# A decoder layer on one Trainium2 core: gate and up by Strassen's seven products

## The chip, the cores and the metric

The kernel runs on one core of one Trainium2 chip. The core has five engines that each run their own list of instructions in order and wait for each other by semaphores: TensorE (PE, matrix products), VectorE (DVE), ScalarE (ACT), GpSimd (POOL) and SyncE (SP), which here only issues transfers. The metric is the device time of one execution in microseconds (us), the median of three runs.

## The reference

One decoder layer on 1024 tokens of width 1024, all in float32: a sub-layer of three token mixers, then a SwiGLU sub-layer. Only SwiGLU is touched:

```
def swiglu(u, w1, w2):
    gate, up = jnp.split(u @ w1, 2, axis=-1)      # w1: 1024 x 5632
    return (jax.nn.silu(gate) * up) @ w2          # w2: 2816 x 1024
...
        u = x * (1.0 + sc2) + sh2
        h = swiglu(u, ffn_w1[l], ffn_w2[l])
        x = layer_norm(DEEPNORM_ALPHA * x + (1.0 + g2) * h, ln2_g[l], ln2_b[l])
```

## The kernel before

Every large product is made from float32 operands split in two parts, high and low: `split` (L106) lets ACT copy the operand to the product's number format (the high part, L107) and lets DVE subtract that from the operand (the low part, L108). A product of two such operands is three matmuls: high by high, high by low, low by high. One matmul is 128x128 weights against 512 columns.

The input of SwiGLU, `u2h` and `u2l`, stands transposed in SBUF: 8 tiles of 128 channels (k), each in two halves of 512 tokens. Gate and up are made in 22 row blocks of 128 hidden channels. For a block, `wblock` loads 1024x128 weights of gate and splits them, and the same for up; `dense` runs, for each k, 3 matmuls on each half of the tokens into a PSUM tile `pgu` of 128x1024. So a block has 2 x 8 x 3 x 2 = 96 matmuls, written from the helper's line L143. Then ACT makes silu of gate (L1073), DVE multiplies with up (L1075), and the block goes to DRAM as part of `s_h` (L1076). Three PSUM tiles named `o0` to `o2` take turns. Block 0 runs its two halves one after the other, since the second half of `u2h` comes last out of the layer norm ahead of it.

Then comes the second product (`accf`, L1114): two groups of 512 tokens, in each 22 steps of k, a step being 24 matmuls on one loaded and split row block of w2 (`w2raw`, L1099) and one of `s_h` (`hraw`, L1104). Its pool `f2a` is opened ahead of the loop over gate and up, with four buffers for the split parts. At its start five rows are spread over all partitions (`g2row`, `l2g`, `l2b`, `l1g`, `l1b`, 512 KB each, on ACT's queue), DVE scales two of them (L1085, L1086), four tiles `x1r` are loaded on SP's queue (L1120), and POOL multiplies and adds on them (L1121, L1122).

The order of the instructions on each engine is set when the program is built: by the order of the code, priorities and a scheduler. `tc.issue_after(last[-1])` ties each group of matmuls behind the one before it. The waits between engines come from which tiles an instruction reads and writes.

Of the kernel before, what the change touches and what calls it, by code (L numbers as in the profile page):

```python
# [17 lines left out]
P = 128  # L18
D = 1024
# [24 lines left out]
def trunk(ctx: ExitStack, tc: tile.TileContext, a: dict, out: bass.AP, scratch: dict):  # L44
# [125 lines left out]
    def half(h):  # L170
        return slice(h * HF, (h + 1) * HF)
# [906 lines left out]
    uctx.close()  # L1078
    with tc.tile_pool(name="f2", bufs=2, reuse_waits="tile") as f2, \
            tc.tile_pool(name="f2l", bufs=4, reuse_waits="tile") as f2l:  # L1080
# [6 lines left out]
        for grp in range(2):  # L1087
            hs = half(grp)
            acc = []
            for t in range(4):  # L1090
                if t < 3:
                    both = pso.tile([P, T], F32, name="accf", tag=f"o{(t + 1) % 3}")
                    acc.append([both[:, half(h)] for h in range(2)])
                else:
                    acc.append([pso.tile([P, HF], F32, name="accf", tag="t", bufs=2) for _ in range(2)])

# [80 lines left out]
```

## Time and profile before

| what | us |
|---|---|
| median of 3 runs | 2154.46 (2154.38 to 2156.28) |
| the profiled execution's own time | 2151.05 |
| its span, first to last instruction | 2149.2 |
| gate and up (`pgu`), first to last matmul's start | 1406.3 to 1885.9 |
| second product (`accf`), first to last matmul's start | 1886.1 to 2136.7 |

The profile is that of one execution. A timeline gives for each instruction when it began and how long it took; a matmul's duration overlaps the next one's, so that the pace of matmuls is read from their starts. In brackets stands how long the engine had stood idle before it, and which instruction released it.

### The profile page before, as it was taken

The numbers are of one execution on the slowest core, as the hardware profiler recorded it, in microseconds if no ns is written. First come the engines' busy times: TensorE is split into PE (matmuls) and PEld (weight loads), VectorE is DVE, ScalarE is ACT, GpSimd is POOL, SyncE is SP. The second block draws the span as 40 slices with busy tenths as digits, with TensorE's granted clock in tenths as the row PEclk, the third lists the DMA queues.
The fourth block names the chain that finished last, engine by engine and source line by source line (L and its number), as shares of the span: only waits on it lengthen the run. The fifth ranks groups of instructions, "written<-read, shape, count | busy, mean of one in ns | idle before, by whom it ended". The sixth has DMA issues, their size and how long they took to land.

```text
span 2149.2 us, 26441 instructions
## 1 busy us (share of the span) xinstructions
PE 2078.0 (97%) x10482; PEld 1637.5 (76%) x10482; DVE 1068.8 (50%) x1986; ACT 688.8 (32%) x1078; POOL 212.6 (10%) x251
## 2 busy tenths in 40 slices
PE   6999999999999999999999999999999999999897
PEld 4777777776777677777767887888888888888786
DVE  6584565645734766445674567532111111154755
ACT  3524323234124342534444324541111111124242
POOL 1101102001010000011121000000000000040803
PEclk9999989989989999999999999999999999999999
DMA  9111111211113454211112755243222222156361
GB/s 285 50 60 37 43 59 35 65 40 35 64 47 94 135 150 118 69 35 38 28 38 88 253 156 172 89 133 93 79 79 69 79 69 79 50 177 194 128 200 65
DMA packets 186923, 202.68 MB, mean 94 GB/s; under 512 B 9500, under 2 KB 144816, under 8 KB 186800
## 3 DMA queue, kind: packets, MB, share of 16 engines
q1 hardware_dynamic: 159216, 133.22, 21.0%
q10 hardware_dynamic: 26752, 66.69, 9.0%
q8 instruction: 82, 1.34, 0.3%
q0 software_dynamic: 832, 1.09, 0.2%
q14 instruction: 41, 0.34, 0.0%
HBM read 162.16 MB, written 38.81 MB: 94 GB/s over the span
## 4 chain that ended last, share of the span: by engine, by line
PE 78%; DVE 10%; issue 4%; ACT 4%; DMA 3%; POOL 1%; SPq 1%; ACTq 0%; DVEq 0%; POOLq 0%
PE pgu L143 22%; PE psd L143 21%; PE accf L1114 9%; PE pj L143 6%; PE woa L1024 3%; PE po L865 2%; PE pt L851 2%; DVE tw L473 1%; DVE TI L475 1%; PE pm L458 1%; PE pss L835 1%; PE pw L525 1%; PE pst L537 1%; PE pss L836 1%; DVE VS L705 1%
## 5 line engine op out<-in xcount | busy, mean ns | idle before, releaser
L143 PE MATMUL psd<-ul,wh 128*128 128x512 f32 x992 | 338.5, 412 | 2.0 <-DVE ul L274 2.0
L107 ACT ACTIVATE wh<-wraw 128x1024 fp32r<-128x1024 f32 (+1 forms) x127 | 124.2, 978 | 663.3 <-PE pgu L143 344.6
L143 PE MATMUL psd<-uh,wh 128*128 128x512 f32 x992 | 334.6, 409 | 0.7 <-ACT uh L272 0.5
L143 PE MATMUL psd<-uh,wl 128*128 128x512 f32 x992 | 332.9, 409 | 1.1 <-DVE wl L120 1.1
L108 DVE TENSOR_TENSOR wl<-wraw,wh 128x1024 fp32r<-128x1024 f32 (+1 forms) x127 | 142.1, 1119 | 214.5 <-ACT wh L107 212.2
L143 PEld LDWEIGHTS psd<-ul,wh 128*128 128x128 f32 x992 | 184.5, 192 | 45.1 <-issue 9.7
L143 PEld LDWEIGHTS psd<-uh,wh 128*128 128x128 f32 x992 | 185.8, 192 | 41.4 <-issue 6.8
L143 PEld LDWEIGHTS psd<-uh,wl 128*128 128x128 f32 x992 | 185.4, 192 | 40.2 <-issue 6.3
L143 PE MATMUL pgu<-oh,wl 128*128 128x512 f32 x352 | 137.2, 390 | 0.0
L143 PE MATMUL pgu<-ul,wh 128*128 128x512 f32 x352 | 137.2, 390 | 0.0
L143 PE MATMUL pgu<-uh,wl 128*128 128x512 f32 x352 | 137.2, 390 | 0.0
L143 PE MATMUL pgu<-uh,wh 128*128 128x512 f32 x352 | 137.2, 390 | 0.0
L143 PE MATMUL pgu<-oh,wh 128*128 128x512 f32 x352 | 137.1, 389 | 0.0
L143 PE MATMUL pgu<-ol,wh 128*128 128x512 f32 x352 | 137.1, 389 | 0.0
L1075 DVE TENSOR_TENSOR ht<-sg,pgu 128x1024 f32<-128x1024 f32 x22 | 26.9, 1221 | 198.8 <-PE pgu L143 179.4
L1114 PE MATMUL accf<-w2h,hh 128*128 128x512 f32 x352 | 116.4, 393 | 6.1 <-DVE t1f L1139 4.5
L1114 PE MATMUL accf<-w2l,hh 128*128 128x512 f32 x352 | 116.7, 395 | 1.2 <-DVE w2l L108 1.2
L1114 PE MATMUL accf<-w2h,hl 128*128 128x512 f32 x352 | 115.9, 392 | 0.0
L1121 POOL TENSOR_TENSOR x1r<-x1r,l1g 128x1024 f32<-128x1024 f32 x8 | 22.1, 2777 | 816.2 <-DVE l1g L1085 742.4
L108 DVE TENSOR_TENSOR w2l<-w2raw,w2h 128x1024 fp32r<-128x1024 f32 x44 | 65.2, 1484 | 37.6 <-ACT w2h L107 37.5
L1114 PEld LDWEIGHTS accf<-w2h,hh 128*128 128x128 f32 x352 | 66.6, 189 | 20.7 <-DVE t1f L1139 4.9
L1114 PEld LDWEIGHTS accf<-w2l,hh 128*128 128x128 f32 x352 | 66.9, 191 | 15.9 <-DVE w2l L108 2.1
(350 smaller groups left out, 3507.0 us busy)
## 6 DMA issues: line engine op xcount, KB each, us to landing
wraw<-in_w_in_dram SPq DMA_DIRECT2D x62, 512.0 KB, 3.9
wraw<-in_ffn_w_dram SPq DMA_DIRECT2D x44, 512.0 KB, 3.9
w2raw<-in_ffn_w_dram SPq DMA_DIRECT2D x44, 512.0 KB, 4.2
wada<-in_w_ada_dram SPq DMA_DIRECT2D x64, 256.0 KB, 3.0
s_gate<-gate ACTq DMA_DIRECT2D x24, 512.0 KB, 2.9
gate<-s_gate ACTq DMA_DIRECT2D x24, 512.0 KB, 4.4
s_h<-ht ACTq DMA_DIRECT2D x22, 512.0 KB, 3.0
hraw<-s_h ACTq DMA_DIRECT2D x44, 256.0 KB, 3.3
```

The source lines that it names most:

```text
L107: S.activation(hi, raw, AF.Copy)
L108: V.tensor_tensor(lo_, raw, hi.bitcast(F32), OP.subtract)
L143: i = mm(ps[:, h * HF:(h + 1) * HF], w[:, k, :], u[k][h], start=(k == 0 and w is wh and u is uh), stop=(k == nk - 1 and w is wl))
L458: mm(pm[hd][:, :, j], BK[hr, c].rearrange("p a b -> p (a b)"), AR[hr, c], start=True, stop=True)
L473: V.tensor_tensor(t3, X[:, s + 1:32, s:s + 1].to_broadcast([64, ni, nj]), TI[:, s:s + 1, 0:nj].to_broadcast([64, ni, nj]), OP.mult)
L475: V.tensor_tensor(TI[:, s + 1:32, 0:nj], TI[:, s + 1:32, 0:nj], t3, OP.add)
L851: PE.transpose(pt[:, j, :], sc[:, (k0 + j) * P:(k0 + j + 1) * P], ident)
L865: mm(po[hr, q0:2 * P], VT[:, kj, hr], PTs[hd][:, kj, q0:2 * P], start=(kj == 0), stop=(kj == nk - 1))
L1024: mm(acc[:, half(h)], m_[k][h2][:, tl], w_[h], start=(k == 0 and m_ is mh and w_ is wh), stop=(k == KT - 1 and m_ is ml))
L1075: V.tensor_tensor(ht, sg, blocks.pop(j)[0], OP.mult)
L1114: mm(acc[t][h], m_[:, t * P:(t + 1) * P], w_[:, half(h)], start=(k == 0 and m_ is hh and w_ is wh), stop=(k == NHB - 1 and m_ is hl))
L1121: G.tensor_tensor(x1, x1, ag, OP.mult)
```

## The change

Blocks 0 and 1 stay as they are. For blocks 2 to 21 gate and up, as a 2x2 matrix product (rows: gate and up; inner: k 0 to 3 and k 4 to 7; columns: the two token halves), are made by Strassen's scheme in the form with shared sums: seven products of 4 x 3 = 12 matmuls, 84 in place of 96.

- Once, beside blocks 0 and 1: three token-side sums (T2, T3, T4, written over tiles that are free or become so, and T1 in new ones), by `minus`, further subtractions and `split`.
- For each block: four weight sums on DVE (L1126 to L1131) and five splits of 512 columns and one of 1024, by `sums`, a generator that is drawn on between the products of the block before.
- Of the seven products the second and the fifth go into `px`, the first, fourth and seventh into `py_`, the third and sixth into `pz`. `px` and `py_` are the two halves of one PSUM tile `pxy` (128x1024), `pz` is a tile of its own. Between the products ACT copies `py_` (L1176) and `px` (L1179) to SBUF, and DVE joins: L1180, L1183, L1186, L1194, L1200; silu and the last products follow (L1191, L1195, L1197, L1201), and two transfers of half a block.
- The first two steps of the second product (AHEAD = 2) are loaded, split and run inside the old pools; the pool `f2a` is opened behind them, when the tiles of gate and up are given back.

```
+    def banks(i):
+        xy = pso.tile([P, T], F32, name="pxy", tag=f"o{i % 3}")
+        return xy[:, 0:HF], xy[:, HF:T], pso.tile([P, HF], F32, name="pz", tag="t", bufs=2)
...
+    def product(ps, w, u, start, stop):
+        with tc.issue_after(last[-1]):
+            for k in range(4):
+                for m, (i, j) in enumerate(((0, 0), (0, 1), (1, 0))):
+                    ins = mm(ps, w[i][:, k, :], u[k][j], start=(start and k == 0 and m == 0),
+                             stop=(stop and k == 3 and m == 2), skip_group_check=not start)
+        last.append(ins.ins)
...
+        a11, a12, a21, a22 = (r[:, 4 * q:4 * q + 4] for r in raw for q in range(2))
+        s1, s2, s3, s4 = (tmp().rearrange("p (k c) -> p k c", k=4) for _ in range(4))
+        V.tensor_tensor(s1, a21, a22, OP.add)
+        V.tensor_tensor(s2, s1, a11, OP.subtract)
+        yield w
+        parts_of(2, s2)
+        V.tensor_tensor(s3, a11, a21, OP.subtract)
+        V.tensor_tensor(s4, a12, s2, OP.subtract)
+        yield w
+        wh = wpool.tile([P, KT, P], F32R, name="wh", tag="wh")
+        wl = wpool.tile([P, KT, P], F32R, name="wl", tag="wl")
+        split(raw[0], wh, wl)
...
+    for k in range(4):
+        t1f.append(minus(B12[k], B11[k]))
+        s_ = tmp()
+        V.tensor_tensor(s_, fp(B22[k][0]), t1f[k], OP.subtract)
+        V.tensor_tensor(s_, s_, fp(B22[k][1]), OP.add)
+        split(s_, *T2[k])
+        t2f.append(s_)
...
+    for i in range(NPL, NHB):
+        gen = sums(raws.pop(i + 1)) if i + 1 < NHB else None
+        px, py_, pz = banks(i)
+        p1, u2_, q_ = [f1.tile([P, HF], F32, name="c", bufs=5) for _ in range(3)]
+        sg = [f1.tile([P, HF], F32, name="ht", bufs=3) for _ in range(2)]
+        product(py_, w[2], T2, True, True)
+        S.activation(u2_, py_, AF.Copy)
+        prepare(gen)
+        product(px, w[11], B11, True, True)
+        S.activation(p1, px, AF.Copy)
+        V.tensor_tensor(u2_, p1, u2_, OP.add)
+        prepare(gen)
+        product(pz, w[1], T1, True, True)
+        V.tensor_tensor(q_, p1, pz, OP.add)
+        prepare(gen)
+        product(py_, w[3], T3, False, True)
+        V.tensor_tensor(q_, q_, py_, OP.add)
+        prepare(gen)
+        if i + 2 < NHB:
+            raws[i + 2] = loads(i + 2)
+        product(px, w[12], B21, False, True)
+        S.activation(sg[0], px, AF.Silu)
+        prepare(gen)
+        product(pz, w[4], B22, False, True)
+        V.tensor_tensor(u2_, u2_, pz, OP.add)
+        S.activation(sg[1], u2_, AF.Silu)
+        nxt = prepare(gen)
+        V.tensor_tensor(sg[1], sg[1], q_, OP.mult)
+        nc.scalar.dma_start(scratch["h"][i * P:(i + 1) * P, half(1)], sg[1])
+        product(py_, w[22], T4, False, True)
+        V.tensor_tensor(p1, p1, py_, OP.add)
+        V.tensor_tensor(sg[0], sg[0], p1, OP.mult)
+        nc.scalar.dma_start(scratch["h"][i * P:(i + 1) * P, half(0)], sg[0])
+        w = nxt
...
+    AHEAD = 2
+    for k in range(AHEAD):
+        raw = wpool.tile([P, D], F32, name="w2raw", tag="wraw")
+        nc.sync.dma_start(raw, w2[k * P:(k + 1) * P, :])
...
+    f1_ctx.close()
+    uctx.close()
     f2a = ctx.enter_context(tc.tile_pool(name="f2a", bufs=4, side="right", reuse_waits="tile"))
-    with tc.tile_pool(name="f1", bufs=2, reuse_waits="tile") as f1:
-        blocks = {}
...
-            else:
-                blocks[j] = block(j)
-                dense(*blocks[j], u2h, u2l, KT)
-            if j % 2:
-                i = j // 2
-                sg = f1.tile([P, T], F32, name="sg")
-                S.activation(sg, blocks.pop(j - 1)[0], AF.Silu)
-                ht = f1.tile([P, T], F32, name="ht")
-                V.tensor_tensor(ht, sg, blocks.pop(j)[0], OP.mult)
-                nc.scalar.dma_start(scratch["h"][i * P:(i + 1) * P, :], ht)
...
-            for k in range(NHB - late):
+            for k in range(0 if grp else AHEAD, NHB - late):
```

What stands in a row on an engine is shown at three places. In these rows the brackets name the semaphores that the instruction waits for, by the engine or the transfer queue (DMAHW) that raises them.

The first place is a block in the middle of gate and up. On PE these rows stood behind each other at a like place, where one half of the tokens follows the other without a wait:

```order
L143 MATMUL pgu_12256<-oh31_9144,wh_12259 128x512
L143 MATMUL pgu_12256<-uh70_118,wh_12259 128x512
L143 MATMUL pgu_12256<-ol31_9146,wh_12259 128x512
L143 MATMUL pgu_12256<-ul70_134,wh_12259 128x512
L143 MATMUL pgu_12256<-oh31_9144,wl_12260 128x512
L143 MATMUL pgu_12256<-uh70_118,wl_12260 128x512
```

Now, in one block, the end of the first product (weights `s2h`, `s2l`, into `py_`) and the start of the second (`wh`, into `px`):

```order
L1103 MATMUL pxy_12404<-uh31_111,s2h_12304 128x512
L1103 MATMUL pxy_12404<-ul31_127,s2h_12304 128x512
L1103 MATMUL pxy_12404<-uh31_111,s2l_12305 128x512
L1103 MATMUL pxy_12404<-oh00_9131,wh_12323 128x512 [waits Activation_49]
L1103 MATMUL pxy_12404<-ol00_9133,wh_12323 128x512
L1103 MATMUL pxy_12404<-oh00_9131,wl_12324 128x512
```

The second product's first matmul waits for ACT; at the start of the fifth product, again into `px`, stands a wait for VectorE:

```order
L1103 MATMUL pxy_12404<-ul71_135,s3h_12365 128x512
L1103 MATMUL pxy_12404<-uh71_119,s3l_12366 128x512
L1103 MATMUL pxy_12404<-oh20_9139,wh_12323 128x512 [waits DVE_49]
L1103 MATMUL pxy_12404<-ol20_9141,wh_12323 128x512
L1103 MATMUL pxy_12404<-oh20_9139,wl_12324 128x512
L1103 MATMUL pxy_12404<-oh21_9140,wh_12323 128x512
```

ACT's rows for one block before were these:

```order
L1076 DMA s_h<-ht 128x1024 [waits DVE_49]
L107 ACTIVATE wh<-wraw 128x1024 [waits DMAHW5_49,PE_49,Activation_49]
L1073 ACTIVATE sg<-pgu 128x1024 [waits PE_49]
L107 ACTIVATE wh<-wraw 128x1024 [waits DMAHW7_49,DVE_49,PE_49]
L1076 DMA s_h<-ht 128x1024 [waits DVE_49]
```

Now they are these, from the end of one block on:

```order
L1202 DMA s_h<-ht 128x512 [waits DVE_49]
L107 ACTIVATE s2h<-s 128x512 [waits PE_49,Activation_49]
L1176 ACTIVATE c<-pxy 128x512 [waits PE_49]
L1179 ACTIVATE c<-pxy 128x512 [waits PE_49]
L107 ACTIVATE s1h<-s 128x512 [waits PE_49,Activation_49]
L107 ACTIVATE s3h<-s 128x512 [waits PE_49,Activation_49]
L107 ACTIVATE wh<-w1raw 128x1024 [waits DMAHW7_49,PE_49]
L1191 ACTIVATE ht<-pxy 128x512 [waits DMAHW1_49,DVE_49,PE_49]
```

The split `s2h` of the next block stands ahead of the copy L1176 of the first product.

The second place is DVE at the start of the Strassen blocks. The rows are of before and of now: before, a block had the rows

```order
L1075 TENSOR_TENSOR ht<-sg,pgu 128x1024 [waits DMAHW2_49,PE_49,Activation_49]
L108 TENSOR_TENSOR wl<-wraw,wh 128x1024 [waits DMAHW7_49,Activation_49]
L108 TENSOR_TENSOR wl<-wraw,wh 128x1024 [waits DVE_49,DMAHW0_49,PE_49,Activation_49]
L1075 TENSOR_TENSOR ht<-sg,pgu 128x1024 [waits DMAHW6_49,PE_49,Activation_49]
L108 TENSOR_TENSOR wl<-wraw,wh 128x1024 [waits DMAHW2_49,Activation_49]
```

and now, in the first Strassen block (`c` is a join's tile, `s` a sum, `s2l`, `wl` low parts of the next block's weights, `ul` a low part of a token sum):

```order
L1127 TENSOR_TENSOR s<-s,w1raw 128x512 [waits DMAHW4_49,DVE_49]
L1180 TENSOR_TENSOR c<-c 128x512
L108 TENSOR_TENSOR ul_126<-s,uh_110 128x512 [waits Activation_49]
L108 TENSOR_TENSOR s2l<-s,s2h 128x512 [waits PE_49,Activation_49]
L1130 TENSOR_TENSOR s<-w1raw 128x512
L1131 TENSOR_TENSOR s<-w1raw,s 128x512
L1183 TENSOR_TENSOR c<-c,pz 128x512 [waits PE_49]
L108 TENSOR_TENSOR wl<-w1raw,wh 128x1024
L1186 TENSOR_TENSOR c<-c,pxy 128x512 [waits DVE_49,PE_49]
```

The L1127 shown is that of block 3. From the one of block 2, the first sum that needs block 2's gate weights, to the join L1186 of block 2, the first on whose end PE waits, there stand 77 instructions on DVE, three of them 1024 wide and the others 512.

The third place is the border to the second product. On DVE before, with `w2l` and `hl` the low parts of a step's operands:

```order
L1075 TENSOR_TENSOR ht<-sg,pgu 128x1024 [waits DMAHW5_49,PE_49,Activation_49]
L1085 TENSOR_SCALAR l1g<-l1g 128x1024 [waits DMAHW0_49]
L108 TENSOR_TENSOR w2l<-w2raw,w2h 128x1024 [waits Activation_49]
L1086 TENSOR_SCALAR l1b<-l1b 128x1024 [waits DMAHW1_49]
L108 TENSOR_TENSOR hl<-hraw,hh 128x512 [waits PE_49,Activation_49]
L108 TENSOR_TENSOR w2l<-w2raw,w2h 128x1024 [waits Activation_49]
L108 TENSOR_TENSOR hl<-hraw,hh 128x512 [waits PE_49,Activation_49]
```

and now:

```order
L1201 TENSOR_TENSOR ht<-ht,c 128x512 [waits DMAHW1_49,DVE_49]
L1246 TENSOR_SCALAR l1g<-l1g 128x1024 [waits DMAHW6_49]
L1247 TENSOR_SCALAR l1b<-l1b 128x1024 [waits DMAHW7_49]
L108 TENSOR_TENSOR hl<-hraw,hh 128x512 [waits DMAHW0_49,DVE_49,Activation_49]
L108 TENSOR_TENSOR w2l<-w2raw,w2h 128x1024 [waits DMAHW1_49,PE_49,Activation_49]
L108 TENSOR_TENSOR hl<-hraw,hh 128x512 [waits DMAHW2_49,Activation_49]
```

Before, the first `w2l` here is that of step 4: those of steps 0 to 3 stand earlier, among the blocks of gate and up. Now it is that of step 2. On SP the load of that step's weights now stands behind the four of `x1r`:

```order
L1227 DMA w2raw<-in_ffn_w_dram 128x1024 [waits DMAHW7_49,DVE_49]
L1269 DMA x1r<-s_n_60 128x1024 [waits DMAHW6_49,PE_49]
L1269 DMA x1r<-s_n_60 128x1024 [waits DMAHW0_49,PE_49]
L1269 DMA x1r<-s_n_60 128x1024 [waits DMAHW3_49]
L1269 DMA x1r<-s_n_60 128x1024 [waits DMAHW5_49]
L1255 DMA w2raw<-in_ffn_w_dram 128x1024 [waits DMAHW1_49]
```

Before, six loads of `w2raw` (steps 0 to 5) stood ahead of the four of `x1r`; now two do.

## Rows read from the trace of the kernel before

**Rows 1.** Head and part 1 of the page: engine, busy us (share), instructions.
```profile
span 2149.2 us, 26441 instructions
...
PE 2078.0 (97%) x10482; PEld 1637.5 (76%) x10482; DVE 1068.8 (50%) x1986; ACT 688.8 (32%) x1078; POOL 212.6 (10%) x251
```

**Rows 2.** Tile pgu: engine op xcount: ns min/median/max, first and last start, forms.
```profile
L143 PE MATMUL pgu<-oh,wh x352: 388/389/393, 1406.3 to 1884.7; 128*128 128x512 f32 x176
...
L143 PE MATMUL pgu<-uh,wl x352: 388/390/390, 1418.7 to 1885.9; 128*128 128x512 f32 x176
```

**Rows 3.** Waits of PE, 1300 us to the end: total us, times, longest.
```profile
PE accf L1114 <- DVE t1f L1139: 4.5, 1, 4.5
```

**Rows 4.** Timeline about a two-half tile: start us, us, engine, line, operation, tiles, [idle].
```profile
1987.22 0.39 PE L1114 MATMUL accf<-w2h,hl 128*128 128x512 f32 x1
...
1989.94 0.39 PE L1114 MATMUL accf<-w2h,hl 128*128 128x512 f32 x1
...
1990.36 1.29 DVE L1139 TENSOR_TENSOR t1f<-accf,g2row 128x512 f32<-128x512 f32 x2 [3.05 <-PE accf L1114]
```

**Rows 5.** Groups by form: shapes xcount | busy us, mean ns | idle before.
```profile
L107 ACT ACTIVATE wh<-wraw 128x1024 fp32r<-128x1024 f32 x103 | 109.1, 1059 | 613.1 <-PE pgu L143 344.6 <-PE psd L143 250.2 <-issue 13.0
...
L856 ACT ACTIVATE PT<-pt 128x512 f32<-128x512 f32 x24 | 14.3, 595 | 20.1 <-PE pt L851 20.1
...
L108 DVE TENSOR_TENSOR wl<-wraw,wh 128x1024 fp32r<-128x1024 f32 x103 | 125.7, 1220 | 211.6 <-ACT wh L107 209.2 <-PE psd L143 2.0
...
L1139 DVE TENSOR_TENSOR t1f<-accf,g2row 128x512 f32<-128x512 f32 x16 | 10.5, 680 | 19.2 <-PE accf L1114 19.2
```

**Rows 6.** Timeline, VectorE and ScalarE: two instructions right behind each other.
```profile
1913.29 0.63 ACT L107 ACTIVATE hh<-hraw 128x512 fp32r<-128x512 f32 x1 [14.54 <-PE accf L1114]
1913.82 1.04 ACT L107 ACTIVATE w2h<-w2raw 128x1024 fp32r<-128x1024 f32 x1
...
1925.06 0.68 DVE L108 TENSOR_TENSOR hl<-hraw,hh 128x512 fp32r<-128x512 f32 x1
...
1925.68 1.23 DVE L108 TENSOR_TENSOR w2l<-w2raw,w2h 128x1024 fp32r<-128x1024 f32 x1
...
1926.86 0.69 DVE L108 TENSOR_TENSOR hl<-hraw,hh 128x512 fp32r<-128x512 f32 x1
```

**Rows 7.** Timeline of PE behind a wait, and windows with the granted clock.
```profile
1320.95 0.50 PE L1024 MATMUL woa<-woh,uh 128*128 128x512 f32 x1 [1.62 <-ACT woh L107]
...
1310.00:1330.00 20.00, 18.38 (x82) 14.86 (x81) 13.66 (x20) 7.59 (x12) 0.00 (x0) 1.00 0.49 156
...
2014.73 0.68 DVE L1139 TENSOR_TENSOR t1f<-accf,g2row 128x512 f32<-128x512 f32 x1
...
2015.47 0.62 PE L1114 MATMUL accf<-w2h,hh 128*128 128x512 f32 x1 [4.51 <-DVE t1f L1139]
...
2015.40:2019.40 4.00, 3.93 (x10) 3.13 (x11) 4.00 (x3) 1.49 (x3) 4.00 (x3) 0.57 0.46 161
```

**Rows 8.** Part 6 of the page: loads of w1, KB, us to landing.
```profile
wraw<-in_ffn_w_dram SPq DMA_DIRECT2D x44, 512.0 KB, 3.9
```

**Rows 9.** Timeline and one window from the end of gate and up.
```profile
1883.55 3.52 SPq L1120 DMA_DIRECT2D x1r<-s_n  x4
...
1899.25 0.69 DVE L1085 TENSOR_SCALAR l1g<-l1g 128x1024 f32<-128x1024 f32 x1 [11.69 <-DMA l1g<-in_ln_g_dram]
...
1900.18 8.75 POOL L1121 TENSOR_TENSOR x1r<-x1r,l1g 128x1024 f32<-128x1024 f32 x3 [742.36 <-DVE l1g L1085]
...
1900.99 2.88 DVE L1086 TENSOR_SCALAR l1b<-l1b 128x1024 f32<-128x1024 f32 x1
1903.80 2.88 DVE L108 TENSOR_TENSOR hl<-hraw,hh 128x512 fp32r<-128x512 f32 x1
1906.60 3.41 DVE L108 TENSOR_TENSOR w2l<-w2raw,w2h 128x1024 fp32r<-128x1024 f32 x1
...
1885.90:1900.00 14.10, 14.10 (x64) 11.69 (x63) 1.98 (x3) 3.16 (x4) 0.00 (x0) 1.00 0.89 308
```

More of the change, by code (lines that the diff above doesn't have):

```diff
@@ new lines, in trunk @@
+    for i in range(NPL):
+        plain = []
+        for part in range(2):
+            c0 = part * HID + i * P
+            plain.append((pso.tile([P, T], F32, name="pgu", tag=f"o{(2 * i + part + 2) % 3}"),
+                          *wblock(w1[:, c0:c0 + P], KT)))
+            dense(*plain[part], u2h, u2l, KT, halves=(0,) if i == 0 else (0, 1))
+        if i == 0:
+            for part in range(2):
+                dense(*plain[part], u2h, u2l, KT, halves=(1,))
+        for h in range(2):
+            ht = f1.tile([P, HF], F32, name="ht", bufs=3)
+            S.activation(ht, plain[0][0][:, half(h)], AF.Silu)
+            V.tensor_tensor(ht, ht, plain[1][0][:, half(h)], OP.mult)
+            nc.scalar.dma_start(scratch["h"][i * P:(i + 1) * P, half(h)], ht)
@@ new lines, in trunk, with loads @@
+    T3 = [(uh[k][1], ul[k][1]) for k in range(4, KT)]
+    T4 = B12
+    def product(ps, w, u, start, stop):
[5 more added lines that the diff above has]
+        last.append(ins.ins)
+    def loads(i):
+        raw = []
+        for part, (pool, tag) in enumerate(((wpool, "wraw"), (gpool, "gate"))):
+            c0 = part * HID + i * P
+            raw.append(pool.tile([P, KT, P], F32, name="w1raw", tag=tag))
+            nc.sync.dma_start(raw[part], w1[:, c0:c0 + P].rearrange("(k p) c -> p k c", p=P))
+        return raw
@@ new lines, in prepare @@
+    def prepare(gen):
+        return next(gen) if gen is not None else None
+    raws = {NPL: loads(NPL), NPL + 1: loads(NPL + 1)}
+    gen = sums(raws.pop(NPL))
+    for _ in range(6):
+        w = next(gen)
+    t1f, t2f = [], []
+    for k in range(4):
[5 more added lines that the diff above has]
+        t2f.append(s_)
+    for k in range(4):
+        split(t1f[k], *T1[k])
@@ new lines, in accumulators, with step @@
+    def accumulators():
+        acc = []
+        for t in range(4):
+            if t < 3:
+                both = pso.tile([P, T], F32, name="accf", tag=f"o{(t + 1) % 3}")
+                acc.append([both[:, half(h)] for h in range(2)])
+            else:
+                acc.append([pso.tile([P, HF], F32, name="accf", tag="t", bufs=2) for _ in range(2)])
+        return acc
+    def step(acc, k, t, ops, halves=(0, 1)):
+        wh, wl, hh, hl = ops
+        for m_, w_ in ((hh, wh), (hh, wl), (hl, wh)):
+            for h in halves:
+                mm(acc[t][h], m_[:, t * P:(t + 1) * P], w_[:, half(h)],
+                   start=(k == 0 and m_ is hh and w_ is wh), stop=(k == NHB - 1 and m_ is hl))
@@ new lines, in trunk @@
+    acc = accumulators()
+    AHEAD = 2
+    for k in range(AHEAD):
+        raw = wpool.tile([P, D], F32, name="w2raw", tag="wraw")
+        nc.sync.dma_start(raw, w2[k * P:(k + 1) * P, :])
+        wh, wl = (wpool.tile([P, D], F32R, name="w2" + m, tag="w" + m) for m in "hl")
+        split(raw, wh, wl)
+        raw = gpool.tile([P, HF], F32, name="hraw", tag="gate")
+        nc.scalar.dma_start(raw, scratch["h"][k * P:(k + 1) * P, half(0)])
+        hh, hl = (f1.tile([P, HF], F32R, name=f"s{2 - k}{m}") for m in "hl")
+        split(raw, hh, hl)
+        with tc.issue_after(last[-1]):
+            for t in range(4):
+                step(acc, k, t, (wh, wl, hh, hl))
@@ L1088, in trunk @@
             hs = half(grp)
[L1089 to L1095, printed above, removed]
+            if grp:
+                acc = accumulators()
             def operands(k, pool):
```

59 lines of the change are left out of this document (40 added, 19 removed).

## The prediction

> **What bounds the kernel now.** I read the head of the page first, for the share of each engine: TensorE is busy 97% of a span of 2149.2 us, VectorE 50%, ScalarE 32% [rows 1]. The profiled execution took 2151.05 us, 1.85 beyond its span and 3.41 below the median; the sum below is made against it, and 3.41 is added at the end.
>
> Then the tile of gate and up. Its six kinds of matmul, 352 each, are 2112; the first starts at 1406.3, the last at 1885.9 [rows 2]. The 2111 steps between fill 479.6 us: 0.2272 each, with some 1.1 us of transposes in it, so 0.2267 a matmul. Each takes 0.39 by itself, so that the next starts 0.16 ahead of its end. In the list of what PE waited for, from 1300 us on, the longest wait is one of 4.5 us, in the second product [rows 3]; `pgu` is in none of its four rows. So in this stage the end is set by the number of matmuls alone, and the other engines wait for PE: an edit there pays its whole matmuls, and any wait it brings PE costs its whole length.
>
> **The change, part by part.**
>
> **A. Matmuls.** 84 in place of 96 for 20 blocks: 240 fewer, at 0.2267: −54.4 us. No other engine could hold this back by volume: a block at 84 x 0.2267 = 19.0 us asks of VectorE 14 instructions of 512 (four sums, five low parts, five joins) at 0.62 from start to start and one of 1024 at 1.18 [rows 6], 9.9 us.
>
> **B. Two waits in each block.** `px` and `py_` are halves of one tile. The trace shows what such a half is worth to a reader: the last matmul into the first half of an `accf` tile started at 1987.22, and VectorE, which reads that half alone, started at 1990.36, right after the last matmul into the second half (1989.94 + 0.39) [rows 4]. It sat idle for 3.05 us though its half had long been done. The tile is one to the waits. In the order this shows the other way round: the second product's first matmul, into `px`, waits for ACT's copy of `py_` (L1176), and the fifth's, into `px` again, for the join L1186, which reads `py_`. PE then cannot write the idle half while the other half is read.
>
> The price, with the last matmul of the product ahead starting at 0:
> - First wait. On ACT the split `s2h` of the next block stands ahead of the copy. It waits for PE too, but for an earlier matmul; I let it start one matmul before the end, at 0.39 − 0.23 + 0.03 = 0.19 (0.03 from a matmul's end to its reader [rows 4]). It takes 0.53 to the next instruction [rows 6]; the copy takes 0.595, by the one PSUM copy of 512 columns that the trace has, `PT` [rows 5]; 0.06 passes to PE (2014.73 + 0.68 to 2015.47), and a matmul after a wait of 1.62 takes 0.50 in place of 0.39, so 0.11 [rows 2, 7]. Less the 0.227 that PE would have taken anyway: 0.19 + 0.53 + 0.595 + 0.06 + 0.11 − 0.227 = 1.26.
> - Second wait. VectorE's join of 512 columns out of PSUM is 0.68 [rows 5]: 0.39 + 0.03 + 0.68 + 0.06 + 0.11 − 0.227 = 1.04.
>
> Together 2.30 a block, 20 blocks: +46.0. From below: ACT's split is done before and nothing restarts slowly, 0.39 + 0.03 + 0.595 + 0.06 − 0.227 = 0.85 and 0.93, so 1.78 or +36. From above: each reader is found in the middle of a 1024-wide instruction (1.06 on ACT, 1.22 on VectorE [rows 5], of which half is left on average, with what is queued behind it): 3.7 or +74. I take 2.30, the sum of the nearest rows. The clock should hold: after the wait of 1.62 the window around it is at 1.00 of 2.4 GHz [rows 7].
>
> The other waits in a block (for the copy L1179, the join L1191, those on `pz`) have at least one product of 12 x 0.227 = 2.7 us between the end of the reading product's matmuls and the wait, against a copy of 0.6, and cost nothing as long as ACT and VectorE are not late.
>
> **C. The first Strassen block.** VectorE has to make block 2's sums and the token sums beside blocks 0 and 1. Count from the first matmul. Block 0's gate ends after 72 matmuls (its halves alternate with up's): 16.3 + 1.1 = 17.4. That frees the split buffers for block 1's gate: 1.06 on ACT, 1.22 on VectorE [rows 5], at 19.7; the load of block 2's gate can then start, 3.9 us [rows 8]: 23.6. From there to the join L1186 of block 2 stand 77 instructions, 74 x 0.62 + 3 x 1.18 = 49.4 [rows 6]: 73.0. PE unstalled would want the fifth product at (192 + 48) x 0.2267 + 1.1 = 55.5. It is 17.5 late; 2.3 of that is already in B, so 15.2; and PE, idle that long, comes back slower: behind its wait of 4.51 the next 4.0 us ran at 0.57 of 2.4 GHz, between the levels of 1.2 and 2.4, which is 4.0 x 0.43 = 1.7 [rows 7]. +17. Bounds: 10, at ScalarE's 0.53 from start to start for the 512-wide ones (23.6 + 39.2 + 3.5 = 66.3); 22, if none overlaps the next (74 x 0.69 + 3 x 1.23 = 54.8, so 78.4) [rows 6].
>
> **D. The border to the second product.** Let E be the end of gate and up (1886.2 before). Before, four steps lay split and two more loaded; now two are split, 2 x 24 x 0.2267 = 10.9 us of cover. Step 2's load stands behind the four `x1r` on SP, its `hraw` behind the five rows on ACT's queue. Before, `x1r` issued at 1883.55, ahead of E, and yet `l1g` on VectorE waited 11.69 for its row and began at 1899.25, E + 13.1; the DMA moved 308 GB/s meanwhile [rows 9]. Now I let one more load of w2 stand ahead of that row, 512 KB at 308 GB/s, 1.7 us: an estimate, E + 14.8. Then VectorE has `l1g`, `l1b`, `hl`, `w2l` of step 2 in this order, beside POOL, whose multiplications and additions start with `l1g`'s end: the first three took 8.75, so eight take some 23.3, to E + 39. Under them `l1b` took 2.88, `hl` 2.88, `w2l` 3.41 [rows 9], in place of 0.69 and 1.23 [rows 6]. From `l1g`'s start to that `w2l`'s end it was 1910.01 − 1899.25 = 10.76, so step 2's is ready at E + 25.6, and those of steps 3 and 4 each 2.88 + 3.41 = 6.29 later, at 31.9 and 38.2. A step on PE is 5.44, and its products with `w2l` begin about 0.4 in: step 2 ends at 30.6, step 3 at 36.9, step 4 at 43.2, where unstalled step 4 would end at 5 x 5.44 = 27.2. That is 16.0, and 1.7 of clock as in C: +18. Bounds: 6, if the rows land earlier (`x1r` is issued later than before, so less is in the way) and VectorE meets less of POOL; 23, if step 5 is late as well.
>
> Nothing else changes on the path: the second group of the second product keeps its code.
>
> **Sum.** −54.4 + 46.0 + 17 + 18 = +26.6. On the profiled execution 2177.7, on the basis of the median 2181.
>
> The Trainium skill, in "PSUM — Partial Sum Buffer", section "PSUM bank collisions raise a hardware error", asks to guard PSUM by bank and quadrant, not by address, and gives a bank as 2 KiB, 512 float32. By that page `px` and `py_` are two banks, and a matmul into one beside a copy of the other would be free: part B would be nothing. [Rows 4] speak against it for this kernel: there VectorE waited for matmuls into a bank that it did not read. What the chip allows and what the program asks for differ here, and the second sets the time.
>
> **The rivals.**
> - **F, halves free of each other: faster.** If PE goes into the second half while the first is read, B is about nothing. Place: the seven product borders of a block; price −54.4 + 17 + 18 = −19.4, so 2135. It decides below (54.4 − 35) / 20 = 0.97 us of waits a block. For it: the two addresses are distinct, and the list of PE's waits is short [rows 3]. Against it: the 3.05 in [rows 4], and the waits named in the order. 0.12.
> - **J, the border hidden.** Rows and loads land early, VectorE outruns POOL: D is 2 in place of 18: 2165. For it: 3.5 us of `x1r` no longer lie against the loads ahead of E. Against it: the 11.69 for `l1g` [rows 9]. 0.14.
> - **Late splits in every block.** ACT or VectorE sit in a 1024 split when PE wants them, B at its upper bound of 74: 2209. For it: `wl` stands directly ahead of L1186 in the first block. Against it: at the pace of 19 us VectorE has half its time free. 0.08.
> - That the 240 matmuls don't leave is excluded: the order has 240 fewer.
>
> **How the numbers follow.** My forecast has 0.62, its own range 2168 to 2194 (B's 36 to 60, C and D each a few us about their value). F 0.12, J 0.14, late splits 0.08, and 0.04 for what I don't see. The range of 8 in 10, 2160 to 2204, takes in J and B up to 69; F and most of the late splits are left out. A measurement of this kernel can tell 0.2% (4.3 us) from no change. Faster: F and 0.02 of the unseen, 0.14. Same: J with B at its lower bound comes to 2155, 0.05. Slower: 0.81.
>
> **What would show it.** A: products of 12 matmuls at 0.2267 from start to start. B: in the waits of PE, tile `pxy` released by ACT's copy L1176 20 times at about 1.26 and by VectorE's L1186 20 times at about 1.04; blocks of 84 matmuls 21.3 us apart (84 x 0.2267 + 2.30), where two blocks of before, at 96, are 21.8. C: PE idle 15 to 18 us in all in the first Strassen block, for VectorE. D: PE idle some 16 us in all in steps 2 to 4 of the second product, for `w2l` and the operands of a step, with a lower granted clock behind the waits. Wrong would be: no wait on `pxy` for L1176 (then F), a block period over 22.7 us (late splits), or PE without a wait in steps 2 to 4 (J).

## The result, and the profile after

The changed kernel took 2178.1 us, median of four runs (2173.76 to 2180.38), against 2154.4 before: a ratio of 1.0107 (1.0089 to 1.0124): 1.1% slower. The profiled execution took 2177.67, 26.6 above that of before, and the forecast's sum was +26.6; but one of its terms was off, and other differences made up for it.

The work is split by three marks in each profile: the first matmul of gate and up, the first of the second product, and the start of its last matmul.

| | before | after | forecast |
|---|---|---|---|
| gate and up starts | 1406.3 | 1409.3 | |
| gate and up | 479.8 | 490.2 (+10.4) | +8.6 (A, B, C) |
| second product | 250.6 | 264.3 (+13.7) | +18 (D) |

The 3.0 us ahead of gate and up are taken as chance: in the profiles of all kernels here that mark lies between 1406.3 and 1418.7, and the two stages alone, 24.1 us longer together, are as much as the medians differ (23.7). The stages are therefore compared by their own length.

Part 1 of the page of the changed kernel answers to [rows 1]: TensorE is 94% busy in place of 97%, VectorE 58% in place of 50%.

```profile
PE 2046.6 (94%) x10242; PEld 1595.4 (73%) x10242; DVE 1262.0 (58%) x2324; ACT 766.8 (35%) x1236; POOL 212.7 (10%) x251
```

The list of PE's waits from 1300 us on (total us, times, longest) answers to [rows 3], where the longest was 4.5 and none stood in gate and up:

```profile
PE pxy L1103 <- DVE c L1186: 24.2, 20, 9.4
PE pxy L1103 <- ACT c L1176: 19.7, 20, 1.0
PE accf L1219 <- ACT w2h L107: 9.1, 2, 7.9
PE accf L1219 <- DVE t1f L1288: 4.7, 1, 4.7
PE accf L1219 <- DVE w2l L108: 3.7, 2, 3.0
PE pxy L1103 <- DVE ht L1077: 2.8, 1, 2.8
```

Both waits of part B are there, twenty times each, and one of L1186 is 9.4 long, in the first Strassen block. A block from its middle, in the timeline (start, us, engine, line, operation, in brackets the idle time before it and its releaser):

```profile
1709.93 0.63 ACT L107 ACTIVATE s2h<-s 128x512 fp32r<-128x512 f32 x1 [2.10 <-PE pxy L1103]
1710.47 0.58 ACT L1176 ACTIVATE c<-pxy 128x512 f32<-128x512 f32 x1
...
1711.10 0.50 PE L1103 MATMUL pxy<-oh,wh 128*128 128x512 f32 x1 [1.04 <-ACT c L1176]
...
1719.60 0.69 DVE L1186 TENSOR_TENSOR c<-c,pxy 128x512 f32<-128x512 f32 x1 [0.70 <-PE pxy L1103]
...
1720.34 0.50 PE L1103 MATMUL pxy<-oh,wh 128*128 128x512 f32 x1 [0.78 <-DVE c L1186]
...
1732.56 0.50 PE L1103 MATMUL pxy<-oh,wh 128*128 128x512 f32 x1 [1.04 <-ACT c L1176]
```

From one block to the next it is 1732.56 − 1711.10 = 21.46 us; the 84 matmuls alone are 19.04. The split `s2h` runs ahead of the copy, as the order said, and PE starts 0.05 after the copy's end and 0.05 after the join's. In three blocks (the first and two near the end) that wait is 0.69.

The first Strassen block:

```profile
1433.10 0.69 DVE L1127 TENSOR_TENSOR s<-s,w1raw 128x512 f32<-128x512 f32 x1 [4.08 <-DMA w1raw<-in_ffn_w_dram]
...
1481.44 0.68 DVE L1186 TENSOR_TENSOR c<-c,pxy 128x512 f32<-128x512 f32 x1
...
1482.17 0.79 PE L1103 MATMUL pxy<-oh,wh 128*128 128x512 f32 x1 [9.42 <-DVE c L1186]
...
1505.80 0.50 PE L1103 MATMUL pxy<-oh,wh 128*128 128x512 f32 x1 [0.78 <-DVE c L1186]
```

VectorE gets its load 23.8 us after the first matmul (forecast 23.6) and ends L1186 at 72.8 (73.0). The windows about it (length; busy and count of PE, PEld, DVE, ACT, POOL; granted clock; DMA share; GB/s) give the clock, ahead of the wait and in it, and for 10 us behind it:

```profile
1453.70:1482.00 28.30, 14.99 (x50) 10.21 (x48) 27.64 (x46) 10.84 (x17) 0.00 (x0) 0.78 0.10 34
...
1482.10:1492.10 10.00, 9.93 (x34) 8.04 (x35) 9.24 (x15) 2.81 (x4) 0.00 (x0) 0.76 0.33 95
```

The border in the timeline (E, the end of gate and up, is 1899.5), answering to [rows 9]:

```profile
1895.64 9.21 SPq L1269 DMA_DIRECT2D x1r<-s_n  x4
...
1910.65 0.82 ACTq L1260 DMA_DIRECT2D hraw<-s_h  x2
1912.74 0.69 DVE L1246 TENSOR_SCALAR l1g<-l1g 128x1024 f32<-128x1024 f32 x1 [11.60 <-DMA l1g<-in_ln_g_dram]
...
1916.85 0.63 ACT L107 ACTIVATE hh<-hraw 128x512 fp32r<-128x512 f32 x1 [18.48 <-DMA hraw<-s_h]
...
1917.51 1.81 DVE L108 TENSOR_TENSOR hl<-hraw,hh 128x512 fp32r<-128x512 f32 x1 [0.95 <-ACT hh L107]
...
1918.47 1.22 PE L1219 MATMUL accf<-w2h,hh 128*128 128x512 f32 x2 [7.91 <-ACT w2h L107]
...
1919.24 3.37 DVE L108 TENSOR_TENSOR w2l<-w2raw,w2h 128x1024 fp32r<-128x1024 f32 x1
...
1922.66 1.22 PE L1219 MATMUL accf<-w2l,hh 128*128 128x512 f32 x2 [2.96 <-DVE w2l L108]
```

The window behind the longer wait:

```profile
1918.40:1926.90 8.50, 5.46 (x12) 3.91 (x13) 8.50 (x4) 2.23 (x4) 8.50 (x4) 0.50 0.34 102
```

PE stops when the two early steps end, and the longer wait is not the one that was forecast: it is for ScalarE, whose `hh` waited for the load `hraw`, and that load was only issued at 1910.65, the moment the early steps' last matmuls ran. For 8.5 us behind it PE has the lower clock level, 0.50, and no wait is left in steps 3 and 4.

The other waits of the second product lie at the change from the first token group to the second:

```profile
2042.43 0.79 PE L1219 MATMUL accf<-w2h,hh 128*128 128x512 f32 x1 [4.69 <-DVE t1f L1288]
...
2068.79 0.73 PE L1219 MATMUL accf<-w2h,hh 128*128 128x512 f32 x2 [1.23 <-ACT w2h L107]
2070.30 1.05 PE L1219 MATMUL accf<-w2l,hh 128*128 128x512 f32 x2 [0.77 <-DVE w2l L108]
```

The kernel before has the same three there, 4.51 at 2015.47 [rows 7] and

```profile
2041.80 0.73 PE L1114 MATMUL accf<-w2h,hh 128*128 128x512 f32 x2 [1.55 <-ACT w2h L107]
2043.38 1.22 PE L1114 MATMUL accf<-w2l,hh 128*128 128x512 f32 x2 [0.84 <-DVE w2l L108]
```

So of the 9.1 and 3.7 in the list above only 7.9 and 3.0 belong to the border; the rest is not the change's.

### The profile page after: what moved, and what is told of

Read it like the earlier page. It is cut to its first block, busy times and chain, and to the rows that moved or that the text cites. A ratio compares the mean times of both kernels' runs of the same rounds, so it can differ in the third digit from the quotient of the medians.

```text
span 2175.9 us, 26614 instructions
## 1 busy us (share of the span) xinstructions
PE 2046.6 (94%) x10242; PEld 1595.4 (73%) x10242; DVE 1262.0 (58%) x2324; ACT 766.8 (35%) x1236; POOL 212.7 (10%) x251
## 4 chain that ended last, share of the span: by engine, by line
PE 73%; DVE 12%; issue 6%; ACT 5%; DMA 3%; POOL 1%; SPq 1%; ACTq 0%; DVEq 0%; POOLq 0%
PE psd L143 20%; PE pxy L1103 13%; PE accf L1219 9%; PE pj L143 6%; PE pz L1103 5%; PE woa L1024 3%; PE po L865 2%; PE pt L851 2%; DVE tw L473 1%; DVE TI L475 1%; PE pm L458 1%; PE pss L835 1%; PE pw L525 1%; PE pst L537 1%; DVE VS L705 1%
## 5 line engine op out<-in xcount | busy, mean ns | idle before, releaser
L107 ACT ACTIVATE wh<-wraw 128x1024 fp32r<-128x1024 f32 (+1 forms) x87 | 81.8, 940 | 325.9 <-PE psd L143 254.0
L108 DVE TENSOR_TENSOR wl<-wraw,wh 128x1024 fp32r<-128x1024 f32 (+1 forms) x87 | 93.1, 1071 | 58.1 <-ACT wh L107 55.8
L1103 PE MATMUL pxy<-oh,wh 128*128 128x512 f32 x160 | 68.0, 425 | 44.0 <-DVE c L1186 24.2
L1103 PEld LDWEIGHTS pxy<-oh,wh 128*128 128x128 f32 x160 | 30.5, 191 | 66.3 <-DVE c L1186 32.7
L1219 PEld LDWEIGHTS accf<-w2h,hl 128*128 128x128 f32 x336 | 64.7, 193 | 13.8
L108 DVE TENSOR_TENSOR hl<-hraw,hh 128x512 fp32r<-128x512 f32 x42 | 43.3, 1036 | 46.5 <-ACT hh L107 46.5
L843 POOL TENSOR_SCALAR sc<-sc,mx 128x128 f32<-128x128 f32 (+7 forms) x64 | 49.0, 769 | 217.9 <-DVE mx L842 181.7
L107 ACT ACTIVATE w2h<-w2raw 128x1024 fp32r<-128x1024 f32 x44 | 46.2, 1052 | 52.8 <-DMA w2raw<-in_ffn_w_dram 27.5
L841 ACT ACTIVATE sc<-sc,mx 128x128 f32<-128x128 f32 (+7 forms) x64 | 49.6, 775 | 42.4 <-DVE mx L840 36.5
```

Source lines behind the costliest of these rows:

```text
L841: S.activation(sc[:, 0:n], sc[:, 0:n], AF.Exp, bias=mx[:, 2:3], accum_out=mx[:, 3:4])
L843: G.tensor_scalar(sc[:, 0:n], sc[:, 0:n], mx[:, 4:5], 1.0, op0=OP.mult, op1=OP.mult)
L1103: ins = mm(ps, w[i][:, k, :], u[k][j], start=(start and k == 0 and m == 0), stop=(stop and k == 3 and m == 2), skip_group_check=not start)
L1219: mm(acc[t][h], m_[:, t * P:(t + 1) * P], w_[:, half(h)], start=(k == 0 and m_ is hh and w_ is wh), stop=(k == NHB - 1 and m_ is hl))
```

## The experiments

Ratios are to the kernel before, on the same chip. The lengths of the two stages are from each run's own profile; the changed kernel has 490.2 and 264.3. The kernel before took 2157.6 beside e1 to e4, 2152.6 beside e5 to e8 and 2158.4 beside e9 to e11, so runs of different groups are compared by ratios or by stages.

The second product is best read in two parts, cut where PE begins to wait for `t1f`, behind the end of the first group: the first part holds the border, the second the group change.

| | up to that wait | from it on |
|---|---|---|
| before | 124.9 | 125.7 |
| changed | 138.2 | 126.1 |
| e2, four early steps | 140.3 | 124.9 |
| e5, rows later | 132.1 | 116.2 |
| e6, no POOL | 135.3 | 126.0 |
| e9, other tiles | 139.0 | 127.8 |
| e10, both | 124.2 | 116.2 |

**e1, two tiles.**

```
-        xy = pso.tile([P, T], F32, name="pxy", tag=f"o{i % 3}")
-        return xy[:, 0:HF], xy[:, HF:T], pso.tile(...)
+        px, py_ = (pso.tile([P, T], F32, name=n, tag=t) for n, t in zip(("px", "py_"), ("o1", "o2" if i % 2 == 0 else "o0")))
+        return px[:, 0:HF], py_[:, 0:HF], pso.tile(...)
```

> px and py_ become two PSUM tiles of their own, all else as in the changed kernel. Theory (the shared tile makes PE wait for the reader of the other half): the 40 waits on L1176 and L1186 of 1.04 and 0.78 us go, a block takes 19.0 us in place of 21.45, about 47 us less than the changed kernel's 2178, so 2131, faster than the kernel before. Rival (PSUM itself is busy with the readers, or VectorE and ScalarE are late and the wait on the tile only stands for it): PE then waits elsewhere in the block, the block stays above 20.5 us and the time above 2160.

2130.68 us, ratio 0.988 (0.9858 to 0.9902); gate and up 439.2, 51.0 shorter, the second product 264.2, the same. All waits on L1176 and L1186 are gone. A window of 100 us in its middle:

```profile
1561.00:1661.00 100.00, 100.00 (x443) 82.81 (x442) 60.82 (x90) 33.72 (x53) 0.00 (x0) 1.00 0.29 89
```

And two of its waits of PE, in the first Strassen block:

```profile
PE pz L1103 <- DVE c L1183: 5.0, 1, 5.0
PE py__11425 L1103 <- DVE ht L1077: 2.5, 1, 2.5
```

PE is busy all the time, while ScalarE and VectorE read the other tile. The theory holds; the rival, in which the readers themselves are the limit, falls. (Two halves of one tile without the wait were not run.) One edit makes the change faster than before. The wait at the start only moved on, from L1186 (9.4) to L1183 (5.0), which with a shorter clock loss is the rest of the 51.0 beyond B's 47.3.

**e2, four early steps.**

```
-    AHEAD = 2
+    AHEAD = 4
-        hh, hl = (f1.tile([P, HF], F32R, name=f"s{2 - k}{m}") for m in "hl")
+        hh, hl = (f1.tile([P, HF], F32R, name=f"s{2 - k % 2}{m}") for m in "hl")
```

> Four steps of the second product in the old pools in place of two (AHEAD = 4), all else as in the changed kernel. Theory (the rows land some 13 us after the end of gate and up, and VectorE is slow beside POOL): the low parts of step 3 now stand behind l1g on VectorE, so PE still waits some 4 us for step 3 and 3 us for step 4, and the gain is about 6: 2172. Rival 1 (only the cover was short: 10.9 us of matmuls): with 21.8 us of cover the waits of 7.9 and 3.0 and the lower clock go altogether, 14 less: 2164. Rival 2 (the transfers at the border are the limit, whatever is ready): the wait moves to step 4, gain under 2.

2183.45, ratio 1.0113 (1.0095 to 1.0130), as the changed kernel; second product 265.2. PE's waits for the operands of a step in it:

```profile
PE accf L1219 <- DVE w2l L108: 6.4, 3, 2.8
PE accf L1219 <- ACT w2h L107: 5.5, 2, 4.9
```

The last 0.6 and 0.9 of them are at the group change. At the border stand 2.8 (`w2l` of step 3), 4.9 and 2.7 (step 4), 10.4 us in place of 10.9: twice the cover bought nothing. Rival 1 falls, and the theory's gain of 6 did not come either. Rival 2 fits the number; why the wait for `w2h` moves along with the last early step was open.

**e3, token sums first.**

```
+    (the loops over T2 and T1, unchanged, moved up to here)
     for _ in range(6):
         w = next(gen)
-    (from here)
```

> The token sums T2 and T1 are written ahead of the weight sums of block 2, all else as in the changed kernel. Theory (VectorE idles some 8 us ahead of the load of block 2's gate weights and then has 77 instructions in a row): 82 instructions now run from 12.2 us after the first matmul without that idle time, L1186 of block 2 ends at 65.5 in place of 72.7, and PE's wait of 9.4 us there becomes about 2.2: 7.5 less, 2171. Rival (the join is late because of what stands close ahead of it, the fourth token sum waiting for the plain blocks and ACT's parts, or the next block's weights): the wait of 9.4 stays above 7 and the time within 2 us of 2178.

2174.62, ratio 1.0075 (1.006 to 1.0091); gate and up 481.3, 8.9 shorter. The two rows of PE's waits that moved:

```profile
PE pxy L1103 <- DVE c L1186: 21.2, 20, 6.4
...
PE pxy L1103 <- DVE ht L1077: 1.5, 1, 1.5
```

The stage gained what was forecast, and L1186 ended 64.7 us after the first matmul (1481.71 + 0.68 − 1417.7; forecast 65.5, the changed kernel 72.8). But the wait there went from 9.4 to 6.4 only, not to 2.2: PE came to it at 58.4 in place of 63.4 us, since the waits ahead of it are shorter (1.5 for 2.8) and the clock in the stretch is 0.88 in place of 0.78. The rival (above 7) falls as well. It is the end of VectorE's list that counts, not the one wait.

**e4, all three** (the first Strassen block's `py_` in `o0`).

> The three edits together: two PSUM tiles (with the first Strassen block in a tile that the plain blocks have long given back), AHEAD = 4, token sums first. Theory (the three costs are at three places and add up): 2178 less 47, less 6, less 7.5, less the wait of 2.8 at the first Strassen block: about 2115. Rival (they hide each other: without the waits in the blocks VectorE's list at the start is late by more, and the border finds fewer weights loaded): less than two thirds of the sum, above 2135.

2125.17, ratio 0.9847 (0.9829 to 0.9865); gate and up 432.0, second product 264.9. In gate and up the edits add up: 58.2 less; the rival (above 2135) falls. At the border nothing came, as in e2: that was 6 us of the forecast, and on this chip the kernel before took 2157.63, 3 us more.

**e5, rows later.** The rows and `x1r`, with what VectorE and POOL do on them, are written behind step 10 of a token group, and tied to its loads. So the edit works at two places: at the border, and at the group change, where the second group's `x1r` stood:

```
+                if k == 10:
+                    with tc.issue_after(sc[-1]), tc.issue_after(sp[-1]):
+                        (first group only: the five rows, l1g and l1b scaled; both groups: the loop over x1r)
```

> The changed kernel with AHEAD = 2 as it is, but the five rows, x1r and what VectorE and POOL do with them are issued behind the loads of step 10 of the second product. Theory (PE waits at the border because the loads of steps 2 and 3 are queued behind 4.5 MB of rows and x1r, and then because l1g, l1b and POOL stand before or beside the splits): step 2 is split about 8 us after the end of gate and up, inside the cover of 10.9; the waits of 7.9, 3.0 and 1.2 us and the lower clock go, and POOL's 23 us later cost nothing, since four steps are then split ahead: 13 us less than the changed kernel. Rival (10.9 us of cover are too short for load, split and low part, whatever else is queued): PE still waits over 6 us before step 2, gain under 6.

2164.24, ratio 1.0047 (1.003 to 1.0064); second product 248.3, 16.0 shorter. By the ratios that is 13 us, the gain forecast, but the number is luck: at the border one wait of 5.0 stays, and most of the gain comes at the group change:

```profile
PE accf L1219 <- ACT w2h L107: 5.0, 1, 5.0
...
PE accf L1219 <- DVE t1f L1292: 0.9, 1, 0.9
```

The timeline of it shows what the wait of 5.0 hangs on (E is 1902.6):

```profile
1913.71 0.81 ACTq L1256 DMA_DIRECT2D hraw<-s_h  x2
1916.95 0.63 ACT L107 ACTIVATE hh<-hraw 128x512 fp32r<-128x512 f32 x1 [15.54 <-DMA hraw<-s_h]
...
2035.57 0.50 PE L1219 MATMUL accf<-w2h,hh 128*128 128x512 f32 x1 [0.92 <-DVE t1f L1292]
```

`hraw` is again issued only as the last early matmuls run (the last weight product of step 1 starts at 1913.2), with nothing ahead of it on its queue: the last transfer there was issued at 1904.22. A reason would be its buffer: in the new pool it can lie over the tile `s1` or `s2` that holds the early steps' hidden rows, and be given back with them. e9 and e10 test that. So neither theory was whole. Of the 16.0 us only 6.1 come at the border (138.2 to 132.1: the waits are 10.9 and 5.0); the other 9.9 come at the group change (126.1 to 116.2), a place that neither theory named: 3.8 of the wait for `t1f`, 2.0 of the two waits behind it, which are gone, the rest in the clock behind them. There POOL multiplied on the second group's `x1r` from 2023.05 on in the changed kernel, and in e5 it does so only behind step 10; what of the 9.9 is POOL's and what the loads' was not tried. The expectation's third wait, of 1.2, was one of the group change too.

**e6, no POOL.** The eight multiplications and additions on `x1r` of the first group are left out, so that its residual stays unscaled.

> The changed kernel without POOL's eight operations on x1r of the first token group, so the residual of that group is left unscaled; loads and rows stay. Theory (the transfers make the first wait, POOL the second): hl and w2l on VectorE at the border take 0.69 and 1.23 in place of 1.8 to 3.4, PE's wait of 3.0 for w2l goes, the wait of 7.9 for step 2's operands stays. Rival (POOL's contention is behind both): both waits shrink below 3 in sum.

2176.42 in one run, so that the stage is read and not the time: second product 261.3, 3.0 shorter. PE's waits for the operands of a step:

```profile
PE accf L1219 <- ACT w2h L107: 9.6, 2, 8.2
...
PE accf L1219 <- DVE w2l L108: 0.7, 1, 0.7
```

VectorE's rows of step 2 in it:

```profile
1919.74 0.69 DVE L108 TENSOR_TENSOR hl<-hraw,hh 128x512 fp32r<-128x512 f32 x1 [1.76 <-ACT hh L107]
1920.68 1.23 DVE L108 TENSOR_TENSOR w2l<-w2raw,w2h 128x1024 fp32r<-128x1024 f32 x1 [0.25 <-ACT w2h L107]
```

VectorE's two splits are back at 0.69 and 1.23 without POOL beside them, and the border's wait for `w2l` is gone (the 0.7 is the one at the group change, where POOL still works, as are 1.4 of the 9.6); the wait of 8.2 behind the load stays. The theory holds, and POOL is worth 3 us of the border.

**e9, e10: the early steps' hidden rows in other tiles**, in the changed kernel (e9) and in e5 (e10).

```
-        hh, hl = (f1.tile([P, HF], F32R, name=f"s{2 - k}{m}") for m in "hl")
+        hh, hl = (f1.tile([P, HF], F32R, name=f"t1{m}{k}") for m in "hl")
```

> The changed kernel, with the split hidden rows of the two early steps in tiles of T1 (free since the third product of the last block) in place of s2 and s1; rows and x1r as they are. Theory of two links in series (the load of step 2's hidden rows waits for the last matmul of the early steps, because its buffer lies over s2 or s1; and the rows are ahead of it in the queue): the load may now issue some 5 us earlier, but behind the rows, and VectorE has l1g in front of hl: the wait of 7.9 shrinks by 3 at most, the time by 0 to 4. Rival (the handed-back tile is the whole of it): waits at the border under 3, 12 less.

> As e9, and the rows and x1r later as in e5. Theory (two links): the wait of 5.0 that e5 left (0.1 to issue, 3.2 to land, 0.5 for hh, 1.2 for w2h, after the last early step) goes as well: border waits under 1, 5 to 6 less than e5, that is 19 less than the changed kernel, ratio to the kernel before about 1.002. Rival (the 10.9 us of cover are short for loads and splits): over 3 us of wait stay.

e9: 2177.0, ratio 1.0086 (1.006 to 1.0112), second product 266.8: no gain. e10: 2157.05, ratio 0.9997 (0.9983 to 1.001), second product 240.4; no wait at the border is left. The timeline of e9 (E is 1898.4) and of e10 (E is 1907.3):

```profile
1905.04 1.84 ACTq L1260 DMA_DIRECT2D hraw<-s_h  x2
...
1916.73 0.63 ACT L107 ACTIVATE hh<-hraw 128x512 fp32r<-128x512 f32 x1 [19.53 <-DMA hraw<-s_h]
```

```profile
1909.30 0.96 ACTq L1256 DMA_DIRECT2D hraw<-s_h  x2
...
2032.37 0.50 PE L1219 MATMUL accf<-w2h,hh 128*128 128x512 f32 x1 [0.92 <-DVE t1f L1292]
```

In e10 the load is issued 2.0 us after E, where e5, with the same queue, issued it at 11.1: only the early steps' tiles are different, so the buffer is what it waited for. In e9 it is issued 6.6 us after E in place of 11.2, and yet `hh` starts no sooner: from the issue to it, behind the rows and `x1r`, it is 11.7 in place of 6.2. So there are two links that end at about the same time, the transfers and the buffer, and cutting one hides what the other is worth: with both cut 14.0 us come back at the border (138.2 to 124.2), 6.1 with the rows alone, nothing with the tiles alone. That is all that the change had cost there (before: 124.9). e10's stage is 7.9 shorter than e5's, 2 more than forecast: 5.0 of wait, the rest with the clock behind it, which was 0.55 in e5 (1918.5 to 1924.5). That e10 comes out level with the kernel before is owed to the group change: gate and up still cost 8.8 more, and 9.5 less there hide it.

**e7, e8, e11: put together.** e7 is e4 with the rows later; e8 writes, for the first Strassen block, the fourth token sum and the next block's weight sums behind the fifth product; e11 adds the tiles of T1.

```
+        if i > NPL:
             prepare(gen)
...
+        if i == NPL:
+            (the loop over T4, moved here)
+            for _ in range(5):
+                prepare(gen)
         product(pz, w[4], B22, False, True)
```

> Two PSUM tiles, token sums first, AHEAD = 4 as in e4, and the rows later as in e5. Theory: e4 less its 12.4 us of waits at the border and 1 us of clock: 2125 becomes 2112. Rival (with rows later the border waits move to where POOL works beside VectorE): above 2119.

> As e7, and in the first Strassen block the fourth token sum and the next block's weights are written behind its fifth product, so that its joins stand some 10 instructions further ahead on VectorE. Theory (what is left at the start, 4.6 us for L1183 and the clock behind it, is order on VectorE): the wait goes, about 5 less than e7: 2107. Rival (volume: VectorE has 60 us of work in the first 65): the wait moves to the seventh product or the next block, within 2 us of e7.

> e8 with the split hidden rows of the early steps in tiles of T1. Theory: the wait of 4.8 for step 4's operands goes, and the lower clock behind it, some 5.5 less than e8: ratio to the kernel before about 0.972. Rival: the wait moves to the following steps, within 2 us of e8.

| | ratio | gate and up | second product |
|---|---|---|---|
| e7 | 0.9783 (0.9763 to 0.9803) | 433.1 | 248.5 |
| e8 | 0.9744 (0.9722 to 0.9766) | 426.2 | 248.3 |
| e11 | 0.9712 (0.9689 to 0.9735) | 426.2 | 240.4 |

e7 is at its forecast by the ratio (2112 of 2157.6 is 0.979), but by another way: its second product is 16.4 shorter than e4's, of which 8.1 come at the group change, while a wait of 4.8 stays at the border. e8's wait for L1183 (4.6 in e7) is gone, and gate and up is 6.9 shorter, so order and not volume held it. e11 is at its forecast and has no wait on VectorE or ScalarE over 0.9 in both stages (the first row lies ahead of them):

```profile
PE woa L1024 <- ACT woh L107: 2.0, 1, 2.0
PE accf L1227 <- DVE t1f L1300: 0.9, 1, 0.9
PE py__11566 L1103 <- DVE s2l L108: 0.4, 1, 0.4
```

It is the fastest version, 2096.33 us where before took 2158.38: gate and up is 53.6 us shorter than before, the 54.4 of 240 matmuls less 0.8. Its second product is 10.2 shorter than before, and that is not Strassen's: 9.5 of it come at the group change (125.7 to 116.2), where the kernel before has the same waits. The rows later in the kernel before, which would show it, were not run.

## Why the prediction was right, and where it was not

- **A** is right: e11, where nothing else is in the way, has the 53.6.
- **B** was forecast at 2.30 a block and 46.0: 21.46 − 19.04 = 2.42, less 0.35 in three blocks, is 47.3. (The idle times, 1.04 and 0.78, are shorter than the prices of 1.26 and 1.04 that the prediction gave as their sign: the price also holds the overlap that is lost and a slower first matmul.) Rival F, halves free of each other, did not come, and e1 shows why: PE can write one accumulator while another engine reads another, but the two halves of one tile are waited for as one. With two tiles F's forecast, 2135, is nearly what e1 took. The Trainium skill, in "PSUM — Partial Sum Buffer", section "PSUM bank collisions raise a hardware error", asks for a guard by bank and quadrant, not by address; e1, where PE is busy 100 us of 100 beside the readers, agrees with it, and the changed kernel waited for more than that.
- **C** was forecast at 17: the fifth product started at 1482.17, 72.9 after the first matmul, where 55.5 was due; 17.4, less 2.1 of the block's own two waits, 15.3; and from there to the next fifth product it was 1505.80 − 1482.17 = 23.63, 2.2 over a block's time, for the clock. 17.5 in all. VectorE's end was forecast to 0.2 us, but the split of the sum was not, and two misses made up for each other: PE idled 13.4 us here (9.4, 2.8, 0.7 and 0.4), 11.9 beyond the block's own waits in place of 15.2, since it was itself slower on the way to the fifth product; and the clock, 0.78 already ahead of the wait, took some 5.6 in place of 1.7. The 2.8, for a tile that the plain blocks still held, was not in the prediction; e4 took it out. e3 and e8 show that the place of the sums in VectorE's list makes C.
- A, B and C give −54.4 + 47.3 + 17.5 = +10.4; measured +10.4.
- **D** is the step that failed: "`hl` 2.88, `w2l` 3.41 … step 2's is ready at E + 25.6 … step 4 at 43.2", +18. `w2l` of step 2 was ready at 1922.61, E + 23.1, and PE waited first, 7.9 us, for ScalarE: the hidden rows' load, not VectorE's list behind `l1g`, ended last, by 0.95 us of idle time on VectorE. Its issue waited for the early steps' last matmul because of the buffer, which the prediction did not look at: it counted queues and engines, but not which memory the new pool takes over. e10 against e5 shows that link, 7.9 us, and e9 that the queue of rows hides it when it stays. The sizes: PE was 11.8 us late when step 2's `w2l` came, in place of 14.3, since it was ready 2.5 earlier. Steps 3 and 4, forecast to add 0.9 each, added nothing: step 3's `w2l` was ready at 1928.69, 1.2 us ahead of the step's start at the lower clock, so that the clock's loss and the late splits lay beside each other, where the sum added them. In all PE idled 10.9 us in place of 16.0, and D is 13.7 in place of 18.
- The 4.3 us too much in D, the 1.8 too little in A to C, and the 3.0 by which gate and up started later in this execution make the sum look better than it was: that +26.6 was met to a tenth is luck. By the medians the change cost 23.7.

## What to carry to other kernels

When matmuls alternate between two accumulators that another engine reads in between, give each its own tile: halves of one tile are waited for as one, and that price is paid at every turn, here 2.4 us of 21.5. Look at the list of the helping engine at the start of a new scheme, not only at its average load, and put ahead what the first block needs. Where one pool takes over another's memory, ask for the first load which old tile lies under it and who reads that last; more steps of cover do not help while that link grows with them, and of two links that end close together both have to be cut before the whole shows. Read a gain at the place where it comes: an edit that meets its forecast may have earned it somewhere else.

## What the runs showed of the hardware

PE kept its full pace (100 us busy out of 100, clock 1.00) with ScalarE and VectorE reading other accumulator tiles between the products [e1]. Waits of 1.0 and 0.8 us twice a block left the granted clock at 1.00 (the windows from 1500 to 1899 us of the changed kernel); behind the wait of 7.9 the window shows 0.50 for 8.5 us, the level of 1.2 GHz, with a further wait of 3.0 in it; behind the wait of 9.4 it shows 0.76 for 10 us, a mean between that level and 2.4, and 2.2 us were lost. VectorE's 1024-wide subtraction took 3.37 beside POOL's multiplications and 1.23 without them [e6].
